# First loads of a hybrid decoder layer: two row blocks of x and of weights in one transfer each, and a tenth warming product

## The chip, the cores and the metric

One core of one Trainium2 chip runs the whole layer. The metric is the device time of one execution in microseconds. The kernel before took 483.64 us (median of 3 runs, 483.13 to 484.74).

## What is computed

One decoder layer on 256 tokens with 1,024 features, all in float32:

```
proj   = x @ w_in + b_in                 # 256x1024 @ 1024x9224, split into
                                         # q_m k_m v_m o_m i_m f_m q_b k_b v_b g_a g_b
h_m    = mlstm(silu(conv(q_m, k_m)), v_m, i_m, f_m)
y_a    = sigmoid(o_m) * head_norm(h_m)
y_b    = moba_attention(q_b, k_b, v_b, rel_bias)
merged = sigmoid(g_a) * (y_a @ w_branch_a) + sigmoid(g_b) * (y_b @ w_branch_b)
x      = layer_norm(ALPHA * x + merged @ w_out)
u      = conv(x @ w_up); x = layer_norm(ALPHA * x + (silu(u_g) * u_up) @ w_down)
```

The change concerns only the first stage, `o_m = x @ w_in[:, o]` (1,024 columns) together with the 8 columns of `i_m` and `f_m`.

## The kernel before

Every float32 matrix is cut into a high and a low part of type float32r: ScalarE casts it (line 91, `wh <- raw`), and VectorE subtracts the cast from it (line 92, `wl <- raw - wh`). Each product is then done as three: high by high, high by low, low by high. TensorE so has three times the products, and they fill nearly all of the time.

The weights come as 1 MB tiles of 128 partitions by 2,048 floats (tensor `wst`), in the order in which they are used, three raw tiles deep. SyncE issues their transfers (line 84). For the first stage the four tiles of the o columns are loaded in smaller pieces. The contraction over 1,024 features is done in eight row blocks of 128 features, k = 0 to 7, and a pair of row blocks is called j = k // 2. For each pair there are

- `load_x(a, b)`, line 210: the columns of transposed x of row blocks a to b-1, 1,024 bytes a partition for each block, 128 KB;
- `load_rows(a, b)`, line 216: the weights' first 512 columns for these row blocks, 2,048 bytes a partition for each block, 256 KB;
- `load_rest(j)`, line 221: the other 512 columns of both row blocks, in two transfers of 256 KB (2,048 bytes a partition each).

Pairs 1 to 3 come with one transfer of x (256 KB) and one of the first columns (512 KB, 4,096 bytes a partition). Pair 0 comes piece by piece: x of block 0, weights of block 0 (the only transfer that is issued by ScalarE, on a queue of its own), x of block 1, weights of block 1.

Then the arithmetic: for k = 0 and 1, `split_x(k, k+1)`, `split_rows(k, k+1)`, `mm_rows(k)`. A `mm_rows` is six products of 128x512 (line 162): x high by w high for two halves of the tokens, x low by w high, x high by w low. After both comes `split_rest(0)` and `mm_rest(0)`: 24 products of 256 or 264 columns (lines 129 to 131). The instructions of each engine stand in the order in which the code is written (`manual_schedule`), so ScalarE casts x 0, w 0, x 1, w 1, then the rest, and TensorE does blocks 0 and 1 back to back if it is not made to wait.

Hardware-queue transfers take eight completion semaphores in turn (`DMAHW0` to `DMAHW7`). A transfer that takes a semaphore for a second time waits on its issuing engine until the transfer that had it before has landed.

Ahead of everything TensorE does nine products of 128x512 on a constant (line 201). Their result is not used; they keep TensorE busy until the first data come.

Of the kernel before, what the change touches and what calls it, by code (L numbers as in the profile page):

```python
# [69 lines left out]
class Kernel:  # L70
# [109 lines left out]
    def run(self):  # L180
        tc, nc, ctx = self.tc, self.nc, self.ctx
# [15 lines left out]

        warm = nc.const_aps.tensor(1.0, [P, 512], BF16)
        wps = self.ps_side([P, 512], "warm_ps")
        for i in range(9):  # L200
            nc.tensor.matmul(wps, warm[:, :P], warm, start=True, stop=True)

        xraw = xp.tile([P, KT, S], F32, tag="xraw", name="xraw")
# [5 lines left out]
        def load_x(a, b):  # L209
            dma(xraw[:, a:b], self.xt_d[:, a:b])  # L210

        def load_rows(a, b, queue=dma):

            j, c = a // 2, a % 4 * 512
            n = (b - a) * 512
            queue(raws[j][:, a % 2 * 512:a % 2 * 512 + n], self.wst[a // 4, :, c:c + n])

        def load_rest(j):

            for c in range(2):  # L220
                dma(raws[j][:, 1024 + c * 512:1536 + c * 512], self.wst[2 + c, :, j * 512:j * 512 + 512])

        def raw_tile():
            raws.append(self.stream.tile([P, 2048], F32, tag="raw", name=f"rawr{len(raws)}", bufs=3))

        for j in range(3):
            raw_tile()
        load_x(0, 1)
        load_rows(0, 1, nc.scalar.dma_start)
        load_x(1, 2)  # L230
        load_rows(1, 2)
        load_rest(0)
        self.wif = xp.tile([P, KT, 8], F32, name="wif")
        dma(self.wif, self.wif_d)
# [1101 lines left out]
```

## Time and profile before

| | |
|---|---|
| median of 3 runs | 483.64 us |
| the profiled execution, its own time | 483.59 us |
| span of the profiled execution, first to last instruction | 481.8 us |
| TensorE busy | 473.1 us (98%) |
| ScalarE busy | 314.4 us (65%) |
| VectorE busy | 368.7 us (77%) |
| DMA, mean over the span | 195 GB/s |

Times in the views count from the first instruction of the span. PE is TensorE's products, PEld its loads of the stationary operand, ACT is ScalarE, DVE VectorE, SP SyncE, and an engine with a q behind it (SPq, ACTq) stands for what its sequencer issues. In a row of the timeline come the start, the duration, the engine, the line, the operation with what it writes and reads, the count, and in brackets the idle time ahead of it with what ended it. Products overlap in their pipeline, so what a product costs a full TensorE is the distance from its start to the next one's start, which is shorter than its duration.

### The profile page before, as it was taken

The page shows a single profiled execution, that of the slowest core. Times are in us where ns is not written, and L with a number is a line of the kernel's source. Part 1 is how long each engine was busy: PE and PEld are TensorE (multiplying, and loading weights), DVE is VectorE, ACT ScalarE, POOL GpSimd, SP SyncE. Part 2 cuts the span into 40 slices and gives each one's busy share as a digit, 9 for nine tenths or more (in the row PEclk, how much of TensorE's full clock was granted, in tenths as well). Part 3 has the DMA queues.
Part 4 walks back from the last instruction along what each step waited for, and adds up shares of the span by engine and source line. Part 5 has one row for each costly group of instructions (what it writes and reads, how often), then busy time and mean ns, then how long its engine had stood idle before and what let it go on. Part 6 is the DMA issues. An engine that isn't in the chain of part 4 may idle for free.

```text
span 481.8 us, 9854 instructions
## 1 busy us (share of the span) xinstructions
PE 473.1 (98%) x4019; PEld 465.2 (97%) x4019; DVE 368.7 (77%) x663; ACT 314.4 (65%) x539; POOL 51.0 (11%) x88
## 2 busy tenths in 40 slices
PE   8999999999999999999999999999999999999994
PEld 5999999999999999999999998999999999999994
DVE  4879986769676977785877789887767766766876
ACT  5676876585658665865765532877776866675771
POOL 0610011010100110002000000021110111010230
PEclk9999999999999999999999999999999999999998
DMA  8976745725663456425964490438655545555202
GB/s 251 389 260 197 218 186 204 265 94 171 215 237 133 139 212 243 163 88 181 354 254 174 175 349 2 174 142 328 232 182 195 226 186 178 186 206 220 88 1 87
DMA packets 18750, 93.76 MB, mean 195 GB/s; under 512 B 4593, under 2 KB 4857, under 8 KB 8849
## 3 DMA queue, kind: packets, MB, share of 16 engines
q1 hardware_dynamic: 14402, 86.82, 49.7%
q0 software_dynamic: 4160, 6.07, 4.1%
q8 instruction: 31, 0.51, 0.4%
q10 hardware_dynamic: 144, 0.26, 0.2%
q14 instruction: 13, 0.11, 0.1%
HBM read 92.05 MB, written 2.63 MB: 197 GB/s over the span
## 4 chain that ended last, share of the span: by engine, by line
PE 90%; DVE 5%; ACT 2%; DMA 1%; issue 1%; SPq 0%; DVEq 0%
PE ffn L1168 9%; PE ps_up L130 7%; PE ps_up L131 7%; PE ps_up L129 7%; PE ps_vm L130 2%; PE ps_vm L129 2%; PE ps_vm L131 2%; PE mix L130 2%; PE ps_wa L130 2%; PE ps_wb L130 2%; PE ps_ga L129 2%; PE ps_gb L129 2%; PE ps_qm L129 2%; PE ps_vb L129 2%; PE ps_qb L129 2%; PE ps_ga L130 2%
## 5 line engine op out<-in xcount | busy, mean ns | idle before, releaser
L92 DVE TENSOR_TENSOR wl<-raw,wh 128x1024 fp32r<-128x1024 f32 x150 | 176.6, 1219 | 27.9 <-ACT wh L91 27.9
L91 ACT CAST wh<-raw 128x1024 fp32r<-128x1024 f32 x150 | 149.5, 1052 | 4.1 <-DMA raw<-in_wst_dram 2.5
L130 PE MATMUL ps_up<-x1l,wh 128*128 128x256 f32 x320 | 88.3, 276 | 0.0
L131 PE MATMUL ps_up<-x1h,wl 128*128 128x256 f32 x320 | 88.3, 276 | 0.0
L129 PE MATMUL ps_up<-x1h,wh 128*128 128x256 f32 x319 | 88.1, 276 | 0.0
L130 PEld LDWEIGHTS ps_up<-x1l,wh 128*128 128x128 f32 x320 | 60.1, 188 | 0.0
L131 PEld LDWEIGHTS ps_up<-x1h,wl 128*128 128x128 f32 x320 | 60.1, 188 | 0.0
L129 PEld LDWEIGHTS ps_up<-x1h,wh 128*128 128x128 f32 x319 | 59.9, 188 | 0.0
L1125 DVE SCALAR_TENSOR_TENSOR cu<-ps_up,vec,cu 128x255 f32<-128x255 f32 (+1 forms) x80 | 33.1, 475 | 21.4 <-ACT cu L1121 21.1
L1168 PE MATMUL ffn<-wh,hh 128*128 128x256 f32 (+1 forms) x171 | 38.0, 280 | 0.0
L1168 PE MATMUL ffn<-wh,hl 128*128 128x256 f32 (+1 forms) x171 | 37.9, 280 | 0.0
L1168 PE MATMUL ffn<-wl,hh 128*128 128x256 f32 (+1 forms) x170 | 37.9, 280 | 0.0
L91 ACT CAST hh<-hf 128x256 fp32r<-128x256 f32 x22 | 9.0, 407 | 38.1 <-DVE hf L1136 38.1
L1168 PEld LDWEIGHTS ffn<-wh,hl 128*128 128x128 f32 x171 | 27.6, 188 | 0.3
L1168 PEld LDWEIGHTS ffn<-wh,hh 128*128 128x128 f32 x171 | 27.7, 188 | 0.2
L1168 PEld LDWEIGHTS ffn<-wl,hh 128*128 128x128 f32 x170 | 27.4, 188 | 0.1
L1175 POOL TENSOR_TENSOR hf<-hf,wsum 128x128 f32<-128x128 f32 x21 | 12.5, 595 | 127.6 <-ACT r L123 127.2
L123 ACT ACTIVATE r<-raw 128x1024 f32<-128x1024 f32 x22 | 23.3, 1059 | 0.3
L1121 ACT ACTIVATE cu<-ps_up,vec 128x256 f32<-128x256 f32 x40 | 16.7, 468 | 8.0 <-PE ps_up L131 7.9
L92 DVE TENSOR_TENSOR hl<-hf,hh 128x256 fp32r<-128x256 f32 x22 | 9.9, 450 | 10.4 <-ACT hh L91 10.4
L129 PE MATMUL mix<-wh,mgh 128*128 128x256 f32 x64 | 17.8, 279 | 0.0
L130 PE MATMUL ps_vm<-wl,xth 128*128 128x256 f32 x64 | 17.8, 278 | 0.0
(327 smaller groups left out, 1484.1 us busy)
## 6 DMA issues: line engine op xcount, KB each, us to landing
raw<-in_wst_dram SPq DMA_DIRECT2D x77, 1024.0 KB, 4.9
rawr<-in_wst_dram SPq DMA_DIRECT2D x9, 256.0 KB, 5.3
lnrow<-in_rows_dram POOLq DMA_DIRECT2D x4, 512.0 KB, 7.7
rawr<-in_wst_dram SPq DMA_DIRECT2D x3, 512.0 KB, 6.1
band<-table POOLq DMA_DIRECT2D x4, 384.0 KB, 13.5
toe<-band POOLq DMA_DIRECT2D x4, 256.0 KB, 3.5
xtok<-in_x_dram POOLq DMA_DIRECT2D x1, 1024.0 KB, 5.1
out_dram<-r SPq DMA_DIRECT2D x4, 256.0 KB, 2.1
```

The lines of the kernel that those rows point to most:

```text
L91: self.nc.scalar.copy(wh, raw)
L92: self.nc.vector.tensor_sub(wl, raw, wh.bitcast(F32))
L123: self.nc.scalar.activation(self.st2[0]["r"], self.down[d][:, i * D:(i + 1) * D], AF.Copy, accum_out=self.wsum[:, k:k + 1])
L129: mm(ps, ah if first is None else first, bh, start=start, stop=False)
L130: mm(ps, ah, bl, start=False, stop=False)
L131: mm(ps, al, bh, start=False, stop=stop)
L1121: act.activation(cu[:, j, :], ps[:, j, :], AF.Copy, scale=tap(2, j))
L1125: v.scalar_tensor_tensor(cu[:, j, o:], ps[:, j, :S - o], tap(t, j), cu[:, j, o:], op0=ALU.mult, op1=ALU.add)
L1168: nc.tensor.matmul(ps[:, lo - a:hi - a], left, right[:, lo:hi], start=k == i == 0, stop=k == NF - 1 and i == 2)
L1175: g.tensor_tensor(h if k else self.hsum, h, w, op=ALU.mult)
```

## The change

Row blocks 0 and 1 of x come in one transfer instead of two (256 KB, 2,048 bytes a partition), on SyncE's queue as before. The first 512 columns of their weights come in one transfer instead of two (512 KB, 4,096 bytes a partition), on ScalarE's queue; before, block 0's came on ScalarE's queue and block 1's on SyncE's. SyncE so issues two transfers fewer ahead of the rest of pair 0. The warming products are ten instead of nine. The arithmetic is as before.

```
-        for i in range(9):
+        for i in range(10):
             nc.tensor.matmul(wps, warm[:, :P], warm, start=True, stop=True)
...
         for j in range(3):
             raw_tile()
-        load_x(0, 1)
-        load_rows(0, 1, nc.scalar.dma_start)
-        load_x(1, 2)
-        load_rows(1, 2)
+        load_x(0, 2)
+        load_rows(0, 2, nc.scalar.dma_start)
         load_rest(0)
```

SyncE's instructions at the start of the program, before (`128x256` is the size of what is loaded, `x2` two of them; `xraw` is x, `rawr` a raw tile of pair 0 or 1, `wif` the weights of the i and f columns; in brackets the semaphores that it waits for, of which `DMAHW0` to `DMAHW7` are the eight):

```order
L210 DMA xraw<-in_xt_dram 128x256 x2
L216 DMA rawr_90<-in_wst_dram 128x512
L221 DMA rawr_90<-in_wst_dram 128x512 x2
L234 DMA wif<-in_wif_dram 128x64
L210 DMA xraw<-in_xt_dram 128x512
L216 DMA rawr_91<-in_wst_dram 128x1024 [waits DMAHW0_49]
L221 DMA rawr_91<-in_wst_dram 128x512 [waits DMAHW1_49]
L221 DMA rawr_91<-in_wst_dram 128x512 [waits DMAHW2_49]
L210 DMA xraw<-in_xt_dram 128x512 [waits DMAHW3_49]
```

The same place in the changed kernel:

```order
L210 DMA xraw<-in_xt_dram 128x512
L221 DMA rawr_91<-in_wst_dram 128x512 x2
L232 DMA wif<-in_wif_dram 128x64
L210 DMA xraw<-in_xt_dram 128x512
L216 DMA rawr_92<-in_wst_dram 128x1024
L221 DMA rawr_92<-in_wst_dram 128x512
L221 DMA rawr_92<-in_wst_dram 128x512 [waits DMAHW0_49]
L210 DMA xraw<-in_xt_dram 128x512 [waits DMAHW1_49]
```

The rest of pair 0 now stands right behind the one transfer of x, and the first wait for a semaphore's second use has moved two transfers back: the second rest of pair 1 waits for `DMAHW0`, which belongs to ScalarE's weight transfer, and pair 2's x for `DMAHW1`, the first x.

ScalarE's first instructions, before (`whr` is the high part of the weights, `xth` that of x):

```order
L216 DMA rawr_90<-in_wst_dram 128x512
L91 ACT_TABLE_LOAD
L91 CAST xth<-xraw 128x256 [waits DMAHW1_49]
L91 CAST whr_134<-rawr_90 128x512 [waits DMAHW0_49]
L91 CAST xth<-xraw 128x256 [waits DMAHW2_49]
L91 CAST whr_134<-rawr_90 128x512 [waits DMAHW3_49]
L91 CAST whr_134<-rawr_90 128x256 [waits DMAHW4_49]
```

And in the changed kernel:

```order
L216 DMA rawr_91<-in_wst_dram 128x1024
L91 ACT_TABLE_LOAD
L91 CAST xth<-xraw 128x256 [waits DMAHW1_49]
L91 CAST whr_133<-rawr_91 128x512 [waits DMAHW0_49]
L91 CAST xth<-xraw 128x256
L91 CAST whr_133<-rawr_91 128x512
L91 CAST whr_133<-rawr_91 128x256 [waits DMAHW2_49]
```

The order of the casts is the same. The casts of block 1 have lost their waits, and the first cast of weights now waits for a transfer of twice the size.

## The prediction

> **What bounds the kernel now.** I read the page's busy shares first, then what TensorE waits for, then TensorE's busy time by stage. The page:
>
> ```profile
> span 481.8 us, 9854 instructions
> PE 473.1 (98%) x4019; PEld 465.2 (97%) x4019; DVE 368.7 (77%) x663; ACT 314.4 (65%) x539; POOL 51.0 (11%) x88
> ```
>
> The waits of TensorE, all of them (total, times, longest):
>
> ```profile
> PE ps_o L162 <- ACT whr L91: 1.3, 2, 0.7
> PE warm_ps L201 <- PEq L1325: 0.8, 1, 0.8
> ```
>
> Busy time by stage (PE first, then PEld, DVE, ACT, POOL, the granted clock, the DMA share, GB/s):
>
> ```profile
> 24.00:100.00 76.00, 76.00 (x659) 75.47 (x658) 62.95 (x129) 53.98 (x89) 6.12 (x8) 1.00 0.61 212
> 100.00:200.00 100.00, 100.00 (x882) 100.00 (x882) 76.40 (x162) 67.34 (x126) 7.78 (x8) 1.00 0.53 184
> 300.00:400.00 100.00, 100.00 (x852) 98.72 (x852) 76.49 (x119) 73.62 (x124) 12.02 (x25) 1.00 0.56 202
> ```
>
> TensorE bounds everything. From 24 us on it is never idle in these stages, and its only waits for data are two at the start, for the first two casts of weights. What the start gains or loses therefore goes to the end one for one, as long as no new wait appears behind it; and the change touches nothing but the start. The chain that ended last begins with the second of these waits (start, duration, what):
>
> ```profile
> 1.24 0.42 SPq L210
> 1.70 4.79 DMA rawr<-in_wst_dram
> 6.52 0.63 ACT whr L91
> 7.19 0.50 PE ps_o L162
> ```
>
> So today the end hangs on block 1's weights, the fourth transfer: issued at 1.70, landed at 6.49, cast at 6.52, used at 7.19. From landing to the first product are 0.70 us. TensorE's timeline around it:
>
> ```profile
> 0.83 3.41 PE L201 MATMUL warm_ps<-const-bfloat16-1.0 128*128 128x512 bf16 x9 [0.83 <-PEq L1325]
> 4.86 0.50 PE L162 MATMUL ps_o<-whr,xth 128*128 128x512 f32 x1 [0.62 <-ACT whr L91]
> 5.20 0.39 PE L162 MATMUL ps_o0b<-whr,xth 128*128 128x512 f32 x1
> 6.12 0.40 PE L162 MATMUL ps_o0b<-wlr,xth 128*128 128x512 f32 x1
> 7.19 0.50 PE L162 MATMUL ps_o<-whr,xth 128*128 128x512 f32 x1 [0.67 <-ACT whr L91]
> 8.68 0.28 PE L129 MATMUL ps_o<-whr,xth 128*128 128x256 f32 x1
> ```
>
> Block 0 starts at 4.86 and its sixth product at 6.12; block 1 could have gone on at 6.35, 0.23 later. It started at 7.19 and was done at 8.68, when the rest of pair 0 begins. Six products after a pause so take 8.68 - 7.19 = 1.49 us, of which 0.34 is the first one's distance to the next (5.20 - 4.86) and 0.23 that of the others: a restart costs 0.11.
>
> **The change part by part.** *The second wait goes.* Block 1's data land with block 0's, so twelve products run without a pause: 1.49 + 1.49 - 0.11 = 2.87 us. If the weight pair lands at L, the first product starts at L + 0.70, and the rest of pair 0 at L + 3.57. Before it was at 8.68. The time so changes by L - 5.11: if the weights still landed early enough for the first product to start at 4.86, the gain would be 8.68 - 4.86 - 2.87 = 0.95 us. That is 0.20% of 483.64 and the most that this change can bring.
>
> *What it costs: the first cast waits for 512 KB instead of 256 KB.* This is the term that decides, and the trace has no such transfer at this place. How fast the DMA engines moved bytes before, by stages (the last column is GB/s):
>
> ```profile
> 1.80:2.50 0.70, 0.70 (x4) 0.16 (x2) 0.00 (x0) 0.70 (x1) 0.00 (x0) 1.00 0.58 180
> 2.50:3.75 1.25, 1.25 (x5) 0.55 (x4) 0.00 (x0) 0.01 (x1) 0.00 (x0) 1.00 1.00 298
> 3.75:5.50 1.75, 1.13 (x6) 0.56 (x4) 1.08 (x3) 1.23 (x3) 0.00 (x0) 1.00 0.94 173
> 5.50:6.50 1.00, 1.00 (x5) 0.49 (x3) 0.37 (x2) 0.00 (x0) 0.00 (x0) 1.00 0.97 332
> 7.50:8.75 1.25, 1.25 (x7) 1.01 (x6) 1.25 (x4) 1.20 (x5) 0.00 (x0) 1.00 1.09 426
> ```
>
> By 3.75 us 0.70 x 180 + 1.25 x 298 = 498 kB had moved. That is close to the first three transfers (524 kB, reached at 3.90 with 26 kB more at 173). The third one, x of block 1, and how the two queues shared the engines (q10 is ScalarE's with w 0, q1 SyncE's with x; issues and packets in two windows):
>
> ```profile
> xraw<-in_xt_dram SPq DMA_DIRECT2D x1, 128.0 KB, 3.1
> ...
> q10 hardware_dynamic: 83, 0.17, 71.3%
> q1 hardware_dynamic: 83, 0.08, 26.7%
> ```
>
> Issued at 1.24 and 3.1 us under way, it landed at 4.34, 0.44 after its last bytes. And the queues took turns packet by packet, 83 against 83, whatever their size.
>
> In the changed kernel x of both blocks (262 kB) and the weights (524 kB) are 786 kB. If 498 kB have moved by 3.75 again, 288 kB of weights are left, in packets of 4,096 bytes, and behind x on SyncE's queue now stands the rest of pair 0 in packets of 2,048: in turns, that is 144 kB more, 432 kB in all. At 426 GB/s it takes 1.01 us: last bytes 4.76, L = 5.20. At the rates that this stretch had (303 kB until 5.50, the other 129 kB at 332 in 0.39) it ends at 5.89, L = 6.33. I take the first: the stretch at 426 is the one where rows of 4,096 bytes moved (pair 1's weights), and the slow one, 173, moved only rows of 2,048. That gives 5.20 - 5.11 = +0.1 us. The bounds of this term are -0.95 and +1.2.
>
> The Trainium skill ("DMA: Bandwidth & Descriptors", Anatomy of one DMA) gives another sum: about 2.0 us fixed plus the bytes at 436 GB/s, fitted on the GpSimd path. Estimated by it, 786 kB issued at 0.79 would land at 4.6. The trace does not bear it out here: the same 768 KB, in four transfers, were complete only at 6.49.
>
> *SyncE's queue.* Two issues fewer stand ahead of the rest of pair 0. In the new order the second rest of pair 1 waits for the weight pair's semaphore, and pair 2's x, its weights and everything later are queued behind it on SyncE. With L near 5.2 this is no later than pair 2's x came before, which waited for w 1 (6.49). Who would notice is ScalarE, with block 2's weights next, and TensorE behind it:
>
> ```profile
> 3.89 0.41 ACT L91 CAST xth<-xraw 128x256 fp32r<-128x256 f32 x1 [1.38 <-DMA xraw<-in_xt_dram]
> 4.20 0.61 ACT L91 CAST whr<-rawr 128x512 fp32r<-128x512 f32 x1
> 6.52 1.96 ACT L91 CAST whr<-rawr 128x512 fp32r<-128x512 f32 x4 [1.40 <-DMA rawr<-in_wst_dram]
> 9.90 1.14 ACT L91 CAST whr<-rawr 128x512 fp32r<-128x512 f32 x2 [0.65 <-DMA rawr<-in_wst_dram]
> ...
> 11.56 0.39 PE L162 MATMUL ps_o<-whr,xth 128*128 128x512 f32 x1
> ```
>
> Block 2's cast starts at 9.90 and is needed at 11.56; it takes 0.7 us to the product, so 0.96 us are to spare. A TensorE that is up to 0.95 earlier still does not meet it. The rest of pair 0 was cast in one go behind w 1 (6.52 to 8.48), so it had landed by then, and is used from 8.68 on; it now comes in no worse a place. I count both at nothing; were the cover gone, each microsecond of lateness would cost one.
>
> *The casts.* ScalarE casts x 0, w 0, x 1, w 1 as before. With all there, w 1 is done about 1.0 us after w 0 (0.4 + 0.6) and needed 1.49 after it: nothing.
>
> *The tenth warming product.* It lies behind the nine, which end at 4.24, and takes at most the distance that they have while the array is slow:
>
> ```profile
> 1.21 0.15 PEld L201 LDWEIGHTS <-const-bfloat16-1.0 128*128 128x128 bf16 x1 [0.28 <-issue]
> 1.64 0.15 PEld L201 LDWEIGHTS <-const-bfloat16-1.0 128*128 128x128 bf16 x1 [0.27 <-issue]
> ```
>
> That is 0.43 us, so it is over by 4.67, while the first product starts at L + 0.70 = 5.9. The idle stretch hides it; without that cover it would cost 0.23 to 0.43. What it might save shows at the end of the trace, where the granted clock fell after the last product:
>
> ```profile
> 474.90 0.28 PE L1168 MATMUL ffn<-wh,hl 128*128 128x256 f32 x1
> ...
> 477.00:478.00 1.00, 0.00 (x0) 0.00 (x0) 0.85 (x3) 0.08 (x1) 0.00 (x0) 0.98 0.00 0
> 478.00:479.00 1.00, 0.00 (x0) 0.00 (x0) 0.72 (x2) 0.00 (x0) 0.00 (x0) 0.50 0.06 23
> ```
>
> The last product ended at 475.18 and the clock was full for most of the microsecond from 477: about 2.8 us of idleness. Between the tenth warming product (over at 4.47 at the full rate) and 5.9 are 1.4 us, so I count nothing. The Trainium skill ("TensorE: Matmul & The Clock Gate", What's actually happening) wants about 3.4 us of an idle window for it and says that the windows run freely. By that rule too the clock would stay up.
>
> Sum: -0.95 (the most that the pause gives back) + 1.05 (the first product from 4.86 to 5.90) = +0.1 us; 483.59 + 0.1 = 483.7 us. The profiled execution lies 1.8 us above its span, and 0.05 below the median of the runs, so it needs no correction.
>
> **The rivals.** *The large rows move at full rate from the start.* Then only the ramp until 2.50 is slow (126 kB), and the other 660 kB, with some 98 kB of the rest in turns, move at 426: 1.78 us, last bytes 4.28, L = 4.72, the time 0.4 us shorter: 483.2 us. For it: the stretch at 426. Against it: 298 in a stretch in which half of the bytes were x. The skill's sum above would put it at 0.5 us shorter.
>
> *The slow stretch comes again.* L = 6.33, +1.2 us: 484.8 us. For it: the same place in time, the same weights read for the first time. Against: rows of 4,096 bytes.
>
> *Slower: the shared engines.* The rest of pair 0 gets as many bytes as the weights, not half as many, since its rows stall. Of the 288 kB only 151 kB move by 5.50 at half of 173, and the other 137 kB at half of 332 take 0.83: last bytes 6.33, L = 6.77, +1.7 us, 485.3 us. It decides from L = 6.56, where the loss passes 1.45 us; from there on TensorE also idles for 2.8 us (4.47 to 7.26), and the clock may fall: twelve products at 0.43 instead of 0.23 add 2.4 us, 487.7 us. Against it: the even turns, 83 and 83.
>
> **How the numbers follow.** A measurement of this kernel can tell about 0.3%, 1.45 us, from no change. The forecast, L from about 4.9 to 5.8, has a chance of 0.50; full rate from the start 0.25; the slow stretch again 0.19; the shared engines 0.06. The first three stay within 1.45 us, at the longest 1.2; what spread of the runs may carry out of it I put at 0.03 on each side. So faster 0.03, same 0.89, slower 0.08. The range goes from the fast rival with some 0.3 us of spread, 482.9, to the slow stretch with 0.2, 485.0, and leaves out the last case.
>
> **What would show it.** In the changed profile: twelve products of line 162 without a pause; one wait of TensorE for line 91 instead of two; the first of them at 5.9 (4.9 to 6.5 is the range); ten warming products ending by 4.7; block 2 at its first product without a wait; the granted clock at 1.00 throughout. I am wrong if the first product starts before 5.2 or after 6.6, if a wait appears at the rest of pair 0 or at block 2, or if the end moves by another amount than the start of the rest of pair 0 does.

## The result and the profile after

| | before | after |
|---|---|---|
| median of 6 runs each, us | 483.57 (483.10 to 484.74) | 487.95 (487.17 to 488.50) |
| ratio to before | | 1.0090, 95% interval 1.0079 to 1.0101 |
| the profiled execution, us | 483.59 | 487.17 |
| span, us | 481.8 | 485.5 |

The changed kernel is 4.4 us slower. The prediction was 483.7 us with a range of 482.9 to 485.0: it was wrong. The profiled execution is the shortest of the six, so the profile shows 3.6 to 3.7 us of the loss and not the other 0.8; what that is made of stays open. All numbers in this section are of that execution.

The page of the changed kernel:

```profile
span 485.5 us, 9850 instructions
PE 475.3 (98%) x4020; PEld 466.6 (96%) x4020; DVE 368.5 (76%) x663; ACT 313.8 (65%) x539; POOL 51.3 (11%) x88
```

TensorE is busy 2.2 us longer, which one product more does not explain. The timeline of TensorE:

```profile
0.83 4.30 PE L201 MATMUL warm_ps<-const-bfloat16-1.0 128*128 128x512 bf16 x10 [0.83 <-PEq L1323]
7.94 0.52 PE L162 MATMUL ps_o<-whr,xth 128*128 128x512 f32 x1 [2.81 <-ACT whr L91]
8.28 0.60 PE L162 MATMUL ps_o0b<-whr,xth 128*128 128x512 f32 x1
8.69 0.63 PE L162 MATMUL ps_o<-whr,xtl 128*128 128x512 f32 x1
9.11 0.63 PE L162 MATMUL ps_o0b<-whr,xtl 128*128 128x512 f32 x1
...
11.93 0.40 PE L162 MATMUL ps_o<-wlr,xth 128*128 128x512 f32 x1
12.16 0.39 PE L162 MATMUL ps_o0b<-wlr,xth 128*128 128x512 f32 x1
12.39 0.28 PE L129 MATMUL ps_o<-whr,xth 128*128 128x256 f32 x1
...
15.27 0.39 PE L162 MATMUL ps_o<-whr,xth 128*128 128x512 f32 x1
...
478.62 0.28 PE L1166 MATMUL ffn<-wh,hl 128*128 128x256 f32 x1
```

Three things are to be seen. There is one pause instead of two, and it ends at 7.94, where it was 4.86. From 8.69 on, the products stand 0.42 apart, not 0.23, until about 11.7. And from the rest of pair 0 on everything is late by the same amount: 12.39 against 8.68 (+3.71), block 2 at 15.27 against 11.56 (+3.71, no wait ahead of it), the last product's start 478.62 against 474.90 (+3.72). The ten warming products end at 5.13; the prediction had them over by 4.7. They stand 0.43 apart for longer, since the clock first comes up at 4.88 in this execution, where it came up at 3.51 before.

The start of the chain that ended last (start, duration, what):

```profile
0.80 6.12 DMA xraw<-in_xt_dram
...
7.34 0.56 ACT whr L91
7.94 0.52 PE ps_o L162
```

Even x, the first and smaller transfer on SyncE's queue, took 6.12 us and landed at 6.92. The weights were cast from 7.3 on. From the first product less 0.70 us, as in the prediction, L = 7.24, where 5.20 was forecast (the view of the issues has the weights 6.5 us under way, landed at about 7.3). How fast bytes moved, and the granted clock in three stretches (same columns as before: the clock third from the end, GB/s last):

```profile
1.80:2.50 0.70, 0.70 (x4) 0.16 (x2) 0.00 (x0) 0.70 (x1) 0.00 (x0) 1.00 0.59 132
2.50:3.75 1.25, 1.25 (x4) 0.45 (x3) 0.00 (x0) 0.01 (x1) 0.00 (x0) 1.00 0.95 172
3.75:5.50 1.75, 1.39 (x4) 0.30 (x2) 0.00 (x0) 0.00 (x0) 0.00 (x0) 1.00 0.90 207
5.50:6.50 1.00, 0.00 (x0) 0.00 (x0) 0.00 (x0) 0.00 (x0) 0.00 (x0) 1.00 0.91 293
7.50:8.75 1.25, 0.81 (x3) 0.66 (x4) 1.13 (x3) 1.25 (x4) 0.00 (x0) 0.82 1.06 410
4.88:8.29 3.41, 0.60 (x3) 0.30 (x3) 0.79 (x2) 1.35 (x4) 0.00 (x0) 1.00 1.02 339
8.30:11.70 3.40, 3.40 (x10) 2.62 (x9) 3.40 (x9) 3.15 (x8) 0.00 (x0) 0.50 1.04 398
11.71:20.00 8.29, 8.29 (x57) 7.69 (x56) 7.81 (x12) 6.61 (x15) 4.76 (x5) 1.00 0.98 362
```

In the stretch from 2.50 to 3.75 the engines were 95% busy and moved 172 GB/s; before it was 298. The clock was 0.50 from 8.30 to 11.70, exactly where the products stand apart. Its changes on record lie 3.41 us apart (up at 4.88, down at 8.30, up at 11.71), and in the other traces, too, the changes lie whole multiples of 3.41 us apart. A stretch of 3.41 us between two such possible changes is a window of the clock in what follows.

The loss at the rest of pair 0 adds up: L - 5.11 = 7.24 - 5.11 = 2.13 us for the late landing, and 4.45 us for twelve products (7.94 to 12.39) where 2.87 were forecast, 1.58 for the clock: 3.71 us. Two questions are open: why the pair landed so late, and why the clock fell.

### The profile page after: what moved, and what is told of

The parts are those of the page before. It is cut to its first block, busy times and chain, and to the rows that moved or that the text cites. A ratio compares the mean times of both kernels' runs of the same rounds, so it can differ in the third digit from the quotient of the medians.

```text
span 485.5 us, 9850 instructions
## 1 busy us (share of the span) xinstructions
PE 475.3 (98%) x4020; PEld 466.6 (96%) x4020; DVE 368.5 (76%) x663; ACT 313.8 (65%) x539; POOL 51.3 (11%) x88
## 3 DMA queue, kind: packets, MB, share of 16 engines
q0 software_dynamic: 4160, 6.07, 4.2%
## 4 chain that ended last, share of the span: by engine, by line
PE 90%; DVE 5%; ACT 2%; DMA 1%; issue 1%; DVEq 0%
PE ffn L1166 9%; PE ps_up L129 7%; PE ps_up L131 7%; PE ps_up L130 7%; PE ps_vm L129 2%; PE ps_vm L130 2%; PE ps_vm L131 2%; PE ps_wb L131 2%; PE mix L130 2%; PE ps_wa L131 2%; PE ps_ga L129 1%; PE ps_gb L129 1%; PE ps_qm L129 1%; PE ps_vb L129 1%; PE ps_ga L130 1%; PE ps_kb L131 1%
```

## The experiments

I began with two theories of the late landing. *Turns*: the queues share the engines packet by packet, and the large packets of the weight pair, or the rest of pair 0 behind x, take time from what is waited for. *Rows*: transfers of these slices are slow at the start for themselves, whoever shares the engines. When the first was not enough, the question became what makes them slow: the young program, memory read for the first time, or the pitch of the rows in memory, for each transfer takes a slice of 1,024 to 4,096 bytes out of rows that lie 8,192 bytes apart, in x and in the weights alike. For the time of the loss that lies in TensorE itself, the theory was the clock. Times are medians, with the ratio to the kernel before as it was measured beside them, and its interval.

**One half of the change: x alone, of before.** Nine warming products, the weights as before.

```
-        load_x(0, 1)
+        load_x(0, 2)
         load_rows(0, 1, nc.scalar.dma_start)
-        load_x(1, 2)
         load_rows(1, 2)
```

> The kernel before with x of row blocks 0 and 1 in one transfer; the weights stay in two (block 0 on ScalarE's queue, block 1 on SyncE's), nine warming products. Theory rows (reads at the start stall when their rows are long, so 2,048-byte rows of x arrive late as 1,024-byte rows did not): x lands past 5 us, first product past 5.5, time 0.5 to 1.5 us above the kernel before. Rival turns (the two queues take turns packet by packet, so that x is held up by as many weight packets as it has itself, and long weight packets hold it up longer): here the weight packets are 2,048 bytes as before, so x lands near 4.3, first product near 5.0, time within 0.3 us of the kernel before.

484.08 us, 1.0013 [1.0001, 1.0024]. The issues of the two first transfers (KB, and us to landing):

```profile
rawr<-in_wst_dram ACTq DMA_DIRECT2D x1, 256.0 KB, 4.1
xraw<-in_xt_dram SPq DMA_DIRECT2D x1, 256.0 KB, 4.0
```

x landed at 4.8, the first product came at 5.76 behind the only wait. The merged x costs some 0.5 us, by the interval between nothing and 1.2. Its landing lies between what the two theories wanted, its first product where *rows* wanted it; it decides little between them.

**The other half: the weights alone, of after.**

```
-        load_x(0, 2)
+        load_x(0, 1)
         load_rows(0, 2, nc.scalar.dma_start)
+        load_x(1, 2)
         load_rest(0)
```

> The changed kernel with x of row blocks 0 and 1 in two transfers again; both blocks' weights stay in one transfer on ScalarE's queue, ten warming products. Theory rows: x in 1,024-byte rows is early again (x 0 before 4.5), the weights in 4,096-byte rows late (6 to 7). Rival turns: x 0 has 8 packets on each engine and lets 8 weight packets of 4,096 pass, so it lands only a little before the weights, past 5. Both: first product at 6.5 to 7.9, time 2 to 4.5 us above the kernel before.

486.40 us, 1.0053 [1.0038, 1.0068]. Its two first issues:

```profile
rawr<-in_wst_dram ACTq DMA_DIRECT2D x1, 512.0 KB, 5.6
xraw<-in_xt_dram SPq DMA_DIRECT2D x1, 128.0 KB, 5.1
```

Block 0's x, 128 KB as before, now took 5.1 us to land; the first product came at 7.12, and the clock was halved from 6.91 to 10.32. Most of the loss comes with the weight pair, and an x that is unchanged in itself is held up by it.

**The clock alone: twenty-two warming products, of after.**

```
-        for i in range(10):
+        for i in range(22):
```

> The changed kernel with 22 warming products instead of ten, which end near 7.6 us. The fall of the granted clock is one part of the loss: twelve products took 4.45 us instead of 2.87, 1.6 us. If TensorE's pause of 2.8 us is what lets it fall, the clock stays at 1.00, the rest of pair 0 begins at 10.8 instead of 12.39, and the time is 1.6 us below the changed kernel, still 2.8 us above the kernel before. If the fall has another cause, no change.

485.84 us, 1.0042 [1.0028, 1.0056], 2.1 us below the changed kernel. Its timeline of TensorE:

```profile
0.83 7.05 PE L201 MATMUL warm_ps<-const-bfloat16-1.0 128*128 128x512 bf16 x22 [0.83 <-PEq L1323]
8.20 0.50 PE L162 MATMUL ps_o<-whr,xth 128*128 128x512 f32 x1 [0.31 <-ACT whr L91]
...
11.07 0.28 PE L129 MATMUL ps_o<-whr,xth 128*128 128x256 f32 x1
```

The first product is no earlier, but from it to the rest are 11.07 - 8.20 = 2.87 us, the forecast's number to the hundredth. So the clock is nearly half of the loss (2.1 of 4.4 us by the medians, 1.58 of 3.71 by the profile of the changed kernel), and keeping TensorE busy takes that part back; the late landing is the rest.

**One queue for all, of after.**

```
-        load_rows(0, 2, nc.scalar.dma_start)
+        load_rows(0, 2)
```

> The changed kernel with the weight pair issued by SyncE behind x instead of by ScalarE; so nothing takes turns with it, x first, then the weights, then the rest. Theory rows: long rows stall as before, 786 kB at about 180 GB/s: x lands at 4 to 5, the weights at 6.5 to 7, time 2 to 4 us above the kernel before. Rival turns: x is alone and lands at 3.3 to 3.9, the weights follow at 5 to 5.5 with no rest of pair 0 between them, first product at 5.7 to 6.2, time within 1 us of the kernel before.

487.70 us, 1.0084 [1.0066, 1.0101]. Windows, as above:

```profile
2.50:3.75 1.25, 1.25 (x4) 0.43 (x3) 0.00 (x0) 0.00 (x0) 0.00 (x0) 1.00 1.06 151
3.75:5.50 1.75, 1.50 (x4) 0.29 (x2) 0.09 (x1) 0.41 (x1) 0.00 (x0) 1.00 0.95 215
```

x, now without a rival, landed at 5.0, but the weights hardly sooner than with two queues (the first product came at 7.84, against 7.94), and the rates are as low. Turns set who lands first, not how much moves.

**The rest of pair 0 held back, of after.** A transfer of 64 bytes that reads the landed weights stands ahead of it on SyncE.

```
         load_rows(0, 2, nc.scalar.dma_start)
+        dma(dram.tile([1, 16], F32, name="held"), raws[0][0:1, 0:16])
         load_rest(0)
```

> The changed kernel with SyncE held until the weight pair has landed (a transfer of 64 bytes from its tile to memory stands ahead of the rest of pair 0). If what made it late is the bytes that shared a slow start (786 kB needed, some 370 kB of the rest moved in between), the weights land near 6.3 instead of 7.2, the first product starts near 7.0, and the time is 0.5 to 2 us below the changed kernel, unless the rest of pair 0 now comes too late (it needs 3 us more). If sharing is not the reason, the weights land at 7.2 again.

486.85 us, 1.0079 [1.0049, 1.0108]. Windows, from the start and at the held transfers:

```profile
2.50:3.75 1.25, 1.25 (x4) 0.44 (x3) 0.00 (x0) 0.01 (x1) 0.00 (x0) 1.00 1.02 218
3.75:5.50 1.75, 1.49 (x4) 0.29 (x2) 0.00 (x0) 0.00 (x0) 0.00 (x0) 1.00 0.69 234
8.00:10.00 2.00, 2.00 (x7) 1.56 (x6) 0.75 (x2) 0.18 (x1) 0.00 (x0) 0.63 0.77 242
```

And block 2 in its timeline of TensorE:

```profile
15.21 0.50 PE L162 MATMUL ps_o<-whr,xth 128*128 128x512 f32 x1 [0.60 <-ACT whr L91]
```

With nothing behind them on the engines, x and the weight pair still moved at 218 to 234 GB/s; the first product came at 7.14, 0.80 earlier than in the changed kernel. So sharing with the rest cost L 0.80 us in these two executions, where the forecast had counted 144 kB at 426 GB/s for it, 0.34 us. Without the sharing the forecast of L would have been 4.87 (288 kB at 426 GB/s from 3.75, and 0.44); here it was 7.14 - 0.70 = 6.44. Of the 2.04 us by which L missed its forecast, about 1.6 are thus the pair's own slowness and about 0.5 the sharing. What was held back then came slowly as well, at 242 GB/s: there is a new wait of 0.60 us at block 2, and the clock was at half from 8.51 to 11.92. Block 2 began at 15.21, only 0.06 earlier than in the changed kernel. The median is 1.1 us below the changed kernel's, but the intervals of the two ratios overlap.

**Is it the young program? Before, with its loads held until 5 us.** This kernel and the next two do work that the reference does not ask for: GpSimd fills the targets of the loads first, so that these have to wait, and unused data are read. Their times say nothing; only the rates count.

```
+        nc.gpsimd.memset(raws[0], 0.0)
+        nc.gpsimd.memset(xraw, 0.0)
+        nc.gpsimd.memset(raws[0][:, 0:512], 0.0)
         load_x(0, 1)
```

> The kernel before, with all loads held back some 5 us by memsets of GpSimd in the tiles that they fill (extra work, same result). In all kernels so far the engines moved 100 to 300 GB/s until 6 us after the start and 350 to 420 from then on, whatever the rows and the queue. Theory young program (something in the program's first 6 us slows transfers): loads that begin at 5.8 run at 350 to 420 GB/s at once. Rival young transfers (the first 4 us of transfers are slow whenever they come): 150 to 250 GB/s from 6 to 10 us, full rate after. Only the profile counts.

489.82 us, one run. Windows:

```profile
5.50:7.00 1.50, 0.00 (x0) 0.00 (x0) 0.00 (x0) 1.25 (x2) 0.00 (x0) 1.00 1.04 204
7.00:9.00 2.00, 0.00 (x0) 0.00 (x0) 0.43 (x1) 0.18 (x1) 0.00 (x0) 0.80 0.82 227
9.00:10.50 1.50, 0.49 (x1) 0.49 (x2) 0.51 (x1) 1.16 (x3) 0.00 (x0) 0.50 1.04 383
```

The same slow stretch, some 3.5 us long, has moved with the loads to 5.5. The time since the start of the program is not its cause.

**Are the engines slow at their first transfers? The same with 1 MB of whole rows read ahead.**

```
+        dma(raws[2], self.wst[45])
+        nc.gpsimd.memset(raws[0], 0.0)
...
         load_x(0, 1)
```

> The same held-back loads, with a transfer of 1 MB of other weights (never used) from the start of the program to fill the time. Theory young program: as without it, full rate from 5.8 on. Rival young transfers: the unused transfer takes the slow 4 us, and the loads behind it run at 350 to 420 GB/s. Second rival, first touch (the first read of a place in memory is slow, whenever it comes): the loads are slow again, 150 to 250 GB/s, after the unused transfer. Only the profile counts.

490.21 us, one run. Windows, first the whole rows and then the slices:

```profile
2.75:5.00 2.25, 2.08 (x5) 0.45 (x3) 0.00 (x0) 0.00 (x0) 2.05 (x2) 1.00 0.93 393
5.25:7.25 2.00, 0.00 (x0) 0.00 (x0) 0.08 (x1) 1.68 (x2) 0.00 (x0) 1.00 0.76 188
7.25:9.25 2.00, 0.00 (x0) 0.00 (x0) 0.35 (x1) 0.35 (x1) 0.00 (x0) 0.81 0.96 251
```

Whole rows of 8,192 bytes, one after the other in memory, run at 393 GB/s from 2.75 us on, where the slices of the changed kernel had 172 to 207. The slices behind them run at 188. GpSimd was filling tiles in both stretches (2.05 of 2.25 us and 1.68 of 2.00), so that is not the difference; SyncE's queue was alone in the first stretch and, until ScalarE's transfer began at 6.37, in the second. It is something in the slices: the pitch of their rows, or that rows and transfers are shorter.

**Are they slow because the memory is read for the first time? The same with these places read ahead as whole rows.**

```
+        dma(raws[2], self.wst[0])
+        dma(raws[1], self.xt_d.rearrange("p k s -> p (k s)"))
...
         load_x(0, 1)
```

> The kernel before with loads held back, and ahead of them two transfers of whole rows that read all of x and the 1 MB tile out of which pair 0's first columns are sliced (into tiles that are filled again later). Theory pitch (a slice at a pitch of 8,192 bytes is slow as such while the transfers start): x 0, x 1, w 0, w 1 are slow again, 150 to 250 GB/s, as with the unrelated 1 MB ahead. Theory first read (only the first slices out of a place not read before are slow): x and w 0, w 1 run at 350 GB/s or more, and only the rest of pair 0, out of two tiles not read before, is slow. Only the profile counts.

493.51 us, one run. Windows:

```profile
2.75:7.25 4.50, 2.08 (x5) 0.44 (x3) 0.00 (x0) 0.00 (x0) 4.50 (x3) 1.00 1.00 424
8.75:10.75 2.00, 0.00 (x0) 0.00 (x0) 0.12 (x1) 1.65 (x2) 0.00 (x0) 0.51 0.71 187
10.75:12.75 2.00, 0.00 (x0) 0.00 (x0) 0.30 (x1) 0.25 (x1) 0.00 (x0) 0.50 0.91 236
```

The first columns of pair 0 and x had been read once at full rate; out of the same places the slices then came at 187. That falls too.

**Compact slices, of after.** The data of pair 0 are given in arrays of their own, packed when the inputs are laid out, so that the rows of one transfer follow each other without a gap. Transfers, sizes and order are those of the changed kernel.

```
-            dma(xraw[:, a:b], self.xt_d[:, a:b])
+            dma(xraw[:, a:b], self.xt_d[:, a:b] if a > 1 else self.x01[a].rearrange("p (k s) -> p k s", s=S))
...
-            queue(raws[j][:, a % 2 * 512:a % 2 * 512 + n], self.wst[a // 4, :, c:c + n])
+            queue(raws[j][:, a % 2 * 512:a % 2 * 512 + n], self.wst[a // 4, :, c:c + n] if a > 1 else self.w01[a])
...
+        "w01": wst[0, :, 0:1024].reshape(P, 1, 1024).transpose(1, 0, 2),
+        "r01": wst[2:4, :, 0:512],
```

> The changed kernel with the same compact arrays (x of both blocks in rows of 2,048 bytes, the weights in rows of 4,096, each transfer contiguous). Theory slices: weights land at 4.5 to 5, first product at 5.2 to 5.7, time within 0.6 us of the kernel before, 4 us below the changed kernel. Rival many transfers: as the changed kernel, first product at 7 to 8.

483.97 us, 1.0007 [0.9998, 1.0016]: 4.0 us below the changed kernel. Windows:

```profile
2.50:3.75 1.25, 1.25 (x4) 0.43 (x3) 0.00 (x0) 0.01 (x1) 0.00 (x0) 1.00 0.74 247
3.75:5.50 1.75, 1.22 (x4) 0.29 (x2) 0.00 (x0) 0.42 (x2) 0.00 (x0) 1.00 1.04 409
```

Its timeline of TensorE (a line was added to this kernel, so that lines 91 and 162 stand as 92 and 163):

```profile
6.07 0.50 PE L163 MATMUL ps_o<-whr,xth 128*128 128x512 f32 x1 [1.10 <-ACT whr L92]
...
8.95 0.28 PE L130 MATMUL ps_o<-whr,xth 128*128 128x256 f32 x1
```

409 GB/s stand where there were 207, the first product comes at 6.07 and the rest at 8.95, with the clock up. The prediction had 5.90 and 8.77; this run's own expectation, 5.2 to 5.7 for the first product, was too early.

**Only the pitch, of after.** Compact arrays change the places as well as the pitch. Here the slices keep their form, but the rows of x and of the o weights are padded: 12,288 bytes apart in one kernel, 8,704 in the other.

```
-            queue(raws[j][:, a % 2 * 512:a % 2 * 512 + n], self.wst[a // 4, :, c:c + n])
+            queue(raws[j][:, a % 2 * 512:a % 2 * 512 + n], self.wpad[a // 4, :, c:c + n])
...
+        "wpad": np.pad(wst[0:4], ((0, 0), (0, 0), (0, 1024))),
```

> The changed kernel, x and the first stage's weights as slices as before, out of arrays whose rows are 12,288 bytes apart instead of 8,192 (4,096 bytes of padding behind each row). Theory pitch (the power of two between the rows of a slice makes the engines meet at the same place in memory): the slices are fast now, the weights land before 5.5, time 2.5 to 4 us below the changed kernel. Rival gaps (a slice is slow because its rows don't follow one another, whatever lies between): as the changed kernel, first product at 7 to 8, within 0.7 us of it.

> The same with rows 8,704 bytes apart (512 bytes of padding). Theory pitch: fast as with 4,096, or faster, since four rows further on no power of two is left either. Rival gaps: as the changed kernel.

12,288 bytes: 483.92 us, 1.0017 [1.0004, 1.0031]; the first product at 6.06. 8,704 bytes: 485.37 us, 1.0038 [1.0026, 1.0049]; at 6.43. Windows of the first:

```profile
2.50:3.75 1.25, 1.25 (x4) 0.43 (x3) 0.00 (x0) 0.01 (x1) 0.00 (x0) 1.00 0.79 305
3.75:5.50 1.75, 1.51 (x4) 0.29 (x2) 0.00 (x0) 0.41 (x2) 0.00 (x0) 1.00 1.03 405
```

And of the second, two windows of the clock:

```profile
3.74:7.15 3.41, 1.55 (x7) 0.83 (x6) 1.17 (x3) 1.71 (x5) 0.00 (x0) 1.00 1.05 399
7.15:10.56 3.41, 3.41 (x10) 2.62 (x9) 3.41 (x8) 3.04 (x9) 0.00 (x0) 0.50 1.03 374
```

A pad of 4,096 bytes alone takes back 3.5 of the 4.4 us by the ratios, 4.0 by the medians, which stand beside different runs of the kernel before. A pad of 512 cures the rates nearly as well (292 and 402 GB/s in the first two windows), but its profiled execution lost the clock once more, after a window in which TensorE was busy 1.55 of 3.41 us. The Trainium skill ("DMA: Bandwidth & Descriptors", Latency and other measured facts) has copies within memory lose half of their rate at a row pitch of 4 MiB and next to nothing at 512 KiB; a pad of 4 KiB restores the rate. The table has no smaller pitch; carried on downwards, it would have 8,192 bytes cost nothing. Here that pitch cost nearly half of the rate from 2.50 to 5.50 us (172 and 207 GB/s against 305 and 405), so the measurement decides; on the pad the two agree. One control is missing: the padded weights, like the compact ones, are an array of their own, and a copy of them at the old pitch was not run. Against the place as the reason stands that three new arrays (compact, 12,288 and 8,704) were all fast.

**All weights of pair 0 in one transfer, of after.** x compact; the 1 MB of weights, first columns and rest, as whole rows.

```
-        load_rows(0, 2, nc.scalar.dma_start)
-        load_rest(0)
+        nc.scalar.dma_start(raws[0], self.w01)
```

> Compact x of both blocks, and all 1 MB of pair 0's weights in one transfer of whole 8,192-byte rows on ScalarE's queue. Theory slices: 1.3 MB at 400 GB/s from 2 us on, landed near 5.7, first product near 6.4 and no wait behind it. Rival many transfers: it is one of few and fast as well, the same. If it is slow too (landing past 7.5), neither the slices nor the number of transfers is the reason, and reading anything from two queues at the start would be left.

486.27 us, 1.0062 [1.0044, 1.0079]. Windows, the rate and the clock's:

```profile
3.00:5.50 2.50, 2.25 (x6) 0.52 (x4) 0.00 (x0) 0.00 (x0) 0.00 (x0) 1.00 1.04 428
5.11:8.52 3.41, 1.70 (x8) 1.28 (x8) 2.00 (x5) 2.57 (x7) 0.00 (x0) 1.00 0.94 300
```

The bytes come at full rate and no wait follows, but the first product waits for all of them until 6.96: a larger first transfer costs its length even at 428 GB/s. The clock stayed up in this execution, with TensorE busy 1.70 of 3.41 us. It was the shortest of four, 485.16 us; whether the others kept the clock is not known.

**Would before gain from the same cure? Pair 0 compact, of before; all four pairs compact, of before and of after.** The edits are those of the compact slices above, for pair 0 or for all pairs.

> The kernel before, with pair 0's x, first columns and rest laid out as arrays of their own, each transfer's rows one behind the other in memory (before: slices of 1,024 or 2,048 bytes out of rows of 8,192). The held-back loads were slow at 6 to 10 us too, while a 1 MB transfer of whole rows ran at 360 to 520 GB/s from 2.75 us on. Theory slices (reads of slices at a pitch of 8,192 bytes are what is slow): the first loads run at 350 GB/s or more from 2.5 us on, w 1 lands before 5, the second wait goes, first product near 4.2: 1 to 1.5 us below the kernel before. Rival many transfers (the first transfers are slow because many are begun and in flight, whatever their layout): as the kernel before, within 0.3 us.

> The kernel before with all four pairs' x, first columns and rest laid out compactly (so far only pair 0's: there the rest of pair 0 began 1.2 us earlier, and a new wait at block 2, whose slices were slow, took it back). Theory slices: the wait at block 2 goes too, no wait is left behind block 0's, time 0.8 to 1.3 us below the kernel before. If the wait at block 2 stays with compact rows, it was the order of the transfers and not the slices: no change.

> The changed kernel (one transfer each, ten warming products) with all four pairs compact. Theory slices: as with pair 0 alone (first product near 6.1), no wait behind: within 0.6 us of the kernel before, and 0.5 to 1.5 us above the compact kernel in the order of before, since the first product needs 786 kB instead of 393. If the one transfer each is the better form once rows are compact: equal to it or below.

Pair 0 of before: 483.48 us, 0.9991 [0.9983, 1.0000]. All pairs of before: 483.63 us beside 484.12 for the kernel before, 0.9988 [0.9979, 0.9998]. All pairs of after: 484.01 us, 1.0002 [0.9987, 1.0016]. The first of these had no pause at block 1, but a new one at block 2:

```profile
11.29 0.50 PE L163 MATMUL ps_o<-whr,xth 128*128 128x512 f32 x1 [0.59 <-ACT whr L92]
```

It had been 1.0 us ahead at the rest of pair 0 (7.65 against 8.68) and was 0.27 ahead here (11.29 against 11.56). The second has no wait at block 2, but in its profile one of 1.16 us at block 1, behind a slow stretch of small compact transfers (first row; the second is the same stretch with pair 0 alone compact):

```profile
3.75:5.50 1.75, 1.47 (x7) 0.81 (x6) 1.26 (x3) 1.19 (x3) 0.00 (x0) 1.00 0.75 163
3.75:5.50 1.75, 1.75 (x7) 0.95 (x6) 1.37 (x3) 1.10 (x4) 0.00 (x0) 1.00 0.79 231
```

I had expected more of it. In this execution, the longest of its twelve (484.15 us), the small transfers of before were no faster compact: 163 GB/s against 173 in this stretch. The same transfers of pair 0 had 231 in the other kernel. So a compact layout did not make the small transfers fast every time, and with one execution of each what else slows them stays open. With all pairs compact, before's order is 0.5 us below the kernel before (by the interval 0.1 to 1.0), which cannot be told from pair 0 alone compact; the merged transfers of the change are not below it.

**The order of the work instead, of before.** The first half of the rest is loaded and used between blocks 0 and 1, in rows of 1,024 bytes.

```
         load_x(0, 1)
         load_rows(0, 1, nc.scalar.dma_start)
+        load_rest_one(0)
...
         load_x(1, 2)
         load_rows(1, 2)
-        load_rest(0)
+        load_rest_one(1)
```

> The kernel before, in another order: x 0, weights 0, the rest of row block 0 (256 KB in one transfer of 1,024-byte rows), then the same of row block 1; the products of block 0 likewise, first columns, then its rest. In a start that gives some 200 GB/s the second step needs 262 kB (rest of block 0) instead of 393 kB (x 1 and weights 1), so its data land 0.5 to 0.8 us earlier than 6.49, and the second wait of TensorE (0.84 us and 0.11 for the restart) shrinks by that or goes: 0.5 to 0.95 us below the kernel before. Rival: short rows or the split rest cost as much as is won: no change.

483.47 us, 1.0003 [0.9993, 1.0013]: no difference. A wait of 0.58 us stands at block 1's products all the same.

## Why the prediction was wrong, point by point

**Where the time is bound: right.** What the start lost went to the end one for one: +3.71 at the rest of pair 0, +3.71 at block 2, +3.72 at the last product. No wait appeared behind the start, the casts of block 1 and the wait on the weight pair's semaphore cost nothing, and the second pause went, as the prediction had it.

**The term that failed first: L.** The step was "If 498 kB have moved by 3.75 again", and then the rest "at 426 GB/s". Neither held: from 1.80 to 3.75 only 0.70 x 132 + 1.25 x 172 = 307 kB moved, and 207 GB/s followed. The rates were those of other transfers at other times: 298 was half x and half weights in shorter pieces, 426 was reached only from 7.50 on. I took "rows of 4,096 bytes" for the reason of the fast stretch; they were slow at the start like the others. I had also set +1.2 as the upper bound, from the slowest stretch of before, as if no new transfer could be slower than an old one. The sum also had x complete by 3.75, so that the rest of pair 0 took the turns behind it. By the prediction's own even turns, x and the weights, 128 packets each, end about together; x landed at 6.92. That slip alone would have made the forecast earlier, not later. L came at 7.24, 2.04 us behind the forecast: about 1.6 of it is the pair's own rate, and about 0.5 the sharing with the rest of pair 0, which cost 0.80 (the run that holds it back) where the forecast had 0.34.

**What made the rates low: shown in part.** Not the queue, not the program's age, not a first read: each of these was changed by itself, the last two on the transfers of the kernel before, and the loads stayed slow. The pitch of 8,192 bytes is shown to be a cause for the merged transfers, since a pad alone brings 405 GB/s and takes back 3.5 to 4.0 us; the control of an unpadded array in another place is missing. How the pitch does it was not shown. That the engines, each at its own rows, meet at the same places in memory would fit, but is only argued, and it leaves open why later slices at the same pitch run at 410 to 426, and why the compact small transfers of before were slow in one execution of two.

**The second term that failed: the clock.** The step was "so I count nothing", for which the idle time was to be 1.4 us. It became 2.8, and the clock fell. The comparison with the end of the trace ("about 2.8 us of idleness") also missed what counts. By the windows of 3.41 us that precede a fall, TensorE was busy 0.60 us (the changed kernel) and 1.55 (rows 8,704 apart), and the clock fell; it was busy 1.70 (one large transfer) and the clock stayed. Between 1.55 and 1.70, close to half of the window, lies what decides in these three. The other traces of the study agree: in no window at whose end the clock fell was TensorE busy for longer, and in none after which it stayed up for less. In the two windows next to the bound all idle time is one pause, of 1.86 and of 1.71 us, so the length of a pause inside a window tells the same; the runs do not separate the two. The Trainium skill ("TensorE: Matmul & The Clock Gate", What's actually happening) asks for a whole idle window; here a window that was 45% busy was enough, so the measurement decides. The prediction priced the fall at 2.4 us and gave it to the rival; it cost 1.58 in the profile, since the clock was down for one window and eight of the twelve products stood 0.2 us further apart (8 x 0.2 = 1.6), and 2.1 in the medians.

**The rival that came nearest** was "the shared engines" with a falling clock, 487.7 us against 487.95 measured. Its mechanism was a part of it: by 7.0 us some 370 to 390 kB of the rest of pair 0 had moved, more than the 288 kB that this rival gave it, but holding the rest back wins only 0.8 us of landing. The near hit of its time is in part luck: L was 0.47 us later than its 6.77, and the fall of the clock cost 0.8 us less than its 2.4. Its chance was too small because the two failures hang together: a landing that is late enough takes the clock as well.

**What the change is worth without the slow start.** With the slices compact or padded to 12,288 bytes, the changed kernel takes 483.92 to 484.01 us, ratios 1.0002 to 1.0017, the intervals from 0.9987 to 1.0031. (Padded to 8,704 bytes, where the profile lost the clock, the ratio is 1.0038.) The forecast's +0.1 us is near to what is left then: with pair 0 compact, the rest of pair 0 began at 8.95, 0.27 us later than before. The pause that goes is paid for by a first product that waits for 786 kB where it had waited for 393.

## What to carry to other kernels

Merging the first transfers of a program makes the first consumer wait for all their bytes: it pays only where the pause that it removes is longer than the time of the added bytes, at a rate that was measured for that very transfer, in that place; the rates of neighbouring transfers are no floor. Slices out of rows 8,192 bytes apart deserve a trial with a padded pitch before transfers are rearranged. And where a landing is uncertain, more warming products insure against a second loss: twelve more won back 2.1 us here (what they cost where the data come early was not measured). In these runs, a TensorE that was busy for less than about half of a 3.41 us window paid for the wait and then for the clock.

## What the runs showed of the hardware

The clock does not always come up at the first chance. In the run with x alone, the products stood 0.43 apart until 9.0 us, though TensorE had been busy 2.64 of the 3.41 us from 2.19 to 5.60; before, it came up with the window from 0.09 to 3.51, busy 2.68. The busy time alone does not decide this: in the changed kernel with all pairs compact the clock stayed down after a window that was busy for 2.77 us (3.09 to 6.50). What does decide it is open. The clock column of the views is no help here: it says 1.00 until the first change on record, also where the products stand 0.43 apart. In the profiled executions of the padded kernel (12,288) and of the changed kernel with all pairs compact it came up only near 9.9 us, and the rest of pair 0 began at 10.70 and 10.61 instead of 8.95. The latter kernel's times fall in two groups, most from 483.7 to 484.1 and some from 485.4 to 486.0: the same 1.7 us, so when the clock comes up may be worth more than the change was forecast to be. (One execution of the second group was profiled, 485.57 us; that the others are late for the same reason is not shown.)

Engines that are nearly always busy can move little: 95% busy at 172 GB/s in the changed kernel, 104% at 428 with whole rows (a share above 100% is the view's own). The share of busy DMA engines is no measure of bytes.
